# Other due times for the small products of attention, and a first down product that may begin with one block

## The chip, the cores and the metric

The kernel runs on one core of a Trainium2 chip. The metric is the device time of one execution in microseconds (us); the profiles show what each engine of that core did: TensorE (PE), VectorE (DVE), ScalarE (ACT), GpSimd (POOL) and SyncE (SP), which issues most transfers. PE runs matrix products into PSUM, which has eight banks of 2 KB per partition; one 128x512 float32 tile fills one.

## The reference

Two layers of a decoder trunk over 256 tokens of width 2048, in float32:

```python
h = rms_norm(x, norm1_g[l])
z = h @ w_in[l]                      # 2048 -> 3584: sgu u | sgu v | q | k | v
z_sgu = gelu(z[..., :2048])
out_a = chunked_sgu(z_sgu, ...)      # v normed per head, 128x128 causal mixing, times u
out_b = swa_sink_attention(q, k, v, ...)   # 16 heads of 64, 4 kv heads, window 128, sinks
mixed = concat([rms_norm(out_a), rms_norm(out_b)])
x = x + mixed @ w_out[l]
h2 = rms_norm(x, norm2_g[l])
x = x + (silu(h2 @ w_gate[l]) * (h2 @ w_up[l])) @ w_down[l]    # 2048 -> 5632 -> 2048
```

## The kernel before

**Products.** Every large product is done three times in a reduced form of float32 so that it keeps float32's precision: `mm3` multiplies the high part of the activations by the high part of the weights, then high by low, then low by high (lines 124 to 126). A weight tile `raw` (128x1024, 512 KB) comes by a transfer on SP into one of seven buffers; ACT casts its high part `wh` (line 94), DVE subtracts to get the low part `wl` (line 95). A `unit` is one such tile and its 12 products of 128x512. All engines work through their queues in order.

**Small work.** Between the units stands small work: transposes on PE (line 188; `ps_t`, `ps_f`, `ps_n` are their PSUM tiles), norms, attention and gating. `later(delay, fn)` puts a function on a list, due at the present `clock` plus the delay; every unit ends with `tick()`, which moves the clock on by one (by 0.5 for a unit of `seven`) and calls what is due, sorted by due time and then by the order in which it was put there. So the delays are the places of small work in the order of the program. A scheduler then settles the order of each engine within what the data allow.

**Banks.** Five PSUM banks are accumulators `acc` (pool `pa`), two are `dacc` (`pd`), one is `sm` (`pm`). Small work asks for a bank through `small_ps`, which takes sm, dacc, dacc, acc in turn. A bank that is asked for again comes free when its last reader, on DVE or ACT, is done.

**Attention.** `attend` makes the scores of one group of heads in two banks (`ps_s0`, `ps_s1`, line 332), which DVE scales and biases into `s` (line 337). One tick later `exps` runs on ACT (lines 353 and 357), later `turn` transposes the probabilities in two more banks (`ps_p`, line 369; ACT copies them to `pt`, line 370), and `weigh` multiplies by the values (`ps_v`, line 381). Six such groups, three for each half of the heads, start at the ticks of `UNIT_AT` (6, 9, 12, 15, 19, 23). `attend_end` transposes a half's output and splits it into `aT` (ACT line 178, DVE line 179). `q_norm` transposes queries in two steps `to_T(0)`, `to_T(1)`. `v_gate` gives the gelu of a half of v (line 434), its squares (line 207), sums on DVE (lines 213 and 169), a power on POOL (line 171), the scaling by it on DVE (lines 439 and 440) and then two spatial products (`ps_g`, line 425). Exp and gelu lie in different function tables of ACT, and a change of table shows as ACT_TABLE_LOAD.

**The feed-forward part.** Ten of eleven blocks of 512 columns go through `seven`, a scheme with seven products of blocks for eight, whose units end in the banks m0 to m4 (all of pool `pa`); ACT's Silu (line 660) and a product on DVE (line 661) then make the two halves m0 and c21 of the block, which are transposed (`ps_f`) and split into `aT` (lines 588 and 589). Block 0 goes through `gate_up`, and all blocks through `down`, in chunks of two or three blocks (`CHUNK`). These two form the second stream, `std_stream`, whose units are mixed with those of `seven` in a fixed ratio of 300 half units to 88 units less a tail of 16. `down` takes its start from the residual: `seed` copies `xres` into a `dacc` bank. When layer 0 ends, `norm_block` transposes the new residual for layer 1.

Of the kernel before, what the change touches and what calls it, by code (L numbers as in the profile page):

```python
# [39 lines left out]
NFF = DFF // NB  # L40
# [3 lines left out]
CHUNK = (2, 3)  # L44
# [19 lines left out]
def trunk(ctx, tc, x, xt, w_in, w_out, w_gate, w_up, w_down, sgu_w, sgu_g, consts,  # L64
# [182 lines left out]
    for lay in range(L):  # L247
# [40 lines left out]
        def q_norm(b, acc, lay=lay, layer=layer, qT=qT):  # L288
            qn = []
            for t in range(NTOK):  # L290
                z = zp.tile([P, NB], F32, tag="z", name="zq")
                nc.scalar.activation(z, acc[t], AF.Copy, scale=layer["rstd1"][t])
                qn.append(z)

            def scaled(inv):
                for t in range(NTOK):
                    z3 = qn[t].rearrange("p (h d) -> p h d", d=HD)
                    nc.vector.tensor_tensor(z3, z3, bc(inv[t], HD), ALU.mult)

            head_inv(qn, 8, scaled)  # L300

            def to_T(c):
                ps = transpose_pair([qn[t][:, 2 * c * P : (2 * c + 2) * P] for t in range(NTOK)])
                nc.scalar.activation(
                    qT[b][:, 2 * c : 2 * c + 2, :], ps, AF.Copy,
                    scale=cst[:, lay, C_QG : C_QG + 1],
                )

            for c in range(2):
                later(4 + c, lambda c=c: to_T(c))  # L310

        ssb = small([P, NTOK, 2], "ssb")
        ob = {}
# [8 lines left out]
        def attend(gp, t, i0, n, zkv=zkv, kT=kT, qT=qT, ob=ob, bias=bias, layer=layer):  # L322
            nk = (t + 1) * P
            nh = 2 * n
            isl = slice(i0, i0 + n)
            nsink = layer["nsink"].rearrange("p (g i) -> p g i", i=GRP)[:, 2 * gp : 2 * gp + 2, isl]
            s = ap.tile([P, 2, n, nk], F32, tag="spt", name="s", bufs=4)
            ps = [small_ps([P, n, nk], f"ps_s{r}") for r in range(2)]
            for i in range(n):
                for r in range(2):  # L330
                    rows = slice(HD * r, HD * r + HD)
                    nc.tensor.matmul(  # L332
                        ps[r][:, i, :], qT[gp][rows, i0 + i, t * P : (t + 1) * P], kT[rows, gp, :nk],
                        start=True, stop=True,
                    )
            for r in range(2):
                nc.vector.scalar_tensor_tensor(
                    s[:, r], ps[r], 1.0 / math.sqrt(HD), bias[2 * gp + r][:, isl, SEQ - nk :],
                    ALU.mult, ALU.add,
                )  # L340

            def row(name):
                return small([P, 2 * GRP], name)[:, :nh].rearrange("p (r i) -> p r i", r=2)

            m, nm, es, den, rden = (row(v) for v in ("m", "nm", "es", "den", "rden"))
            nc.vector.tensor_reduce(m, s, AX.X, ALU.max)
            nc.vector.scalar_tensor_tensor(nm, m, -1.0, nsink, ALU.mult, ALU.min)
            nc.vector.tensor_tensor(es, nm, nsink, ALU.subtract)

            def exps():  # L350
                for r in range(2):
                    for i in range(n):
                        nc.scalar.activation(
                            s[:, r, i], s[:, r, i], AF.Exp, bias=nm[:, r, i : i + 1],
                            accum_out=den[:, r, i : i + 1],
                        )
                nc.scalar.activation(es, es, AF.Exp)

            s8 = s.rearrange("p r i (b k) -> p (r i b) k", k=P)

            pts = []

            def turn():
                pt = ap.tile([P, 8, P], F32, tag="spt", name="pt", bufs=4)
                pts.append(pt)
                for half in range(2):
                    pst = small_ps([P, 4, P], "ps_p")
                    for i in range(4):
                        nc.tensor.transpose(pst[:, i, :], s8[:, 4 * half + i, :], ident)
                    nc.scalar.copy(pt[:, 4 * half : 4 * half + 4], pst)  # L370

            def weigh():
                pt = pts[0]
                nc.vector.tensor_tensor(rden, den, es, ALU.add)
                nc.vector.reciprocal(rden, rden)
                pv = small_ps([P, 2, n, HD], "ps_v")
                for r in range(2):
                    cols = slice((NKV + 2 * gp + r) * HD, (NKV + 2 * gp + r + 1) * HD)
                    for i in range(n):
                        for b in range(t + 1):  # L380
                            nc.tensor.matmul(  # L381
                                pv[:, r, i], pt[:, (r * n + i) * (t + 1) + b, :], zkv[b][:, cols],
                                start=b == 0, stop=b == t,
                            )
                if (gp, t) not in ob:
                    ob[gp, t] = zp.tile([P, NB], F32, tag="z", name="ob")
                o4 = ob[gp, t].rearrange("p (r i d) -> p r i d", r=2, d=HD)[:, :, isl]
                nc.vector.tensor_tensor(
                    o4, pv, rden.unsqueeze(3).to_broadcast([P, 2, n, HD]), ALU.mult
                )  # L390

            later(1, exps)
            later(3, turn)
            later(5, weigh)

        def attend_end(gp, r, lay=lay, ob=ob, ssb=ssb, pairs_b=pairs_b):
# [9 lines left out]
        def v_gate(b, acc, lay=lay, layer=layer, gate=gate):  # L406
            wm = ap.tile([P, 8, P], F32, tag="big", name="wm", bufs=8)
            with tc.issue_after(layer["anchor"].ins):
                nc.gpsimd.dma_start(wm, sgu_w[lay, :, 8 * b : 8 * b + 8, :])
            nc.gpsimd.affine_select(  # L410
                out=wm, in_=wm, pattern=[[0, 8], [1, P]], compare_op=ALU.is_ge, fill=0.0,
                base=0, channel_multiplier=-1,
            )
            gb = zp.tile([P, NB], F32, tag="z", name="gb")
            nc.gpsimd.dma_start(gb, sgu_g[lay, b * NB : (b + 1) * NB].partition_broadcast(P))

            v = ap.tile([P, NTOK, NB], F32, tag="big", name="v", bufs=8)
            vh = v.rearrange("p c (h d) -> p h c d", d=HD)
            gate[b] = v

            def spatial(half):
                hs = slice(4 * half, 4 * half + 4)
                ps = small_ps([P, 4, NTOK, HD], "ps_g")
                for h in range(4):
                    nc.tensor.matmul(
                        ps[:, h], wm[:, 4 * half + h, :], vh[:, 4 * half + h],
                        start=True, stop=True,
                    )
                sb = cst[:, lay, C_SB + 8 * b + 4 * half : C_SB + 8 * b + 4 * half + 4]
                for t in range(NTOK):  # L430
                    nc.vector.tensor_tensor(vh[:, hs, t], ps[:, :, t], bc(sb, HD), ALU.add)

            for t in range(NTOK):
                nc.scalar.activation(v[:, t], acc[t], AF.Gelu, scale=layer["rstd1"][t])

            def scaled(inv):
                for t in range(NTOK):
                    v3 = v[:, t].rearrange("p (h d) -> p h d", d=HD)
                    nc.vector.tensor_tensor(v3, v3, bc(inv[t], HD), ALU.mult)
                    nc.vector.tensor_tensor(v[:, t], v[:, t], gb, ALU.mult)  # L440

            head_inv([v[:, t] for t in range(NTOK)], 8, scaled)
            for half in range(2):
                later(6 + half, lambda half=half: spatial(half))

        ssa = small([P, NTOK, 2], "ssa")
        pairs_a = []
# [80 lines left out]
        for i, (gp, t, i0, n) in enumerate(units):  # L528
            at = UNIT_AT[i]
            later(at, lambda gp=gp, t=t, i0=i0, n=n: attend(gp, t, i0, n))  # L530
            if i % 3 == 2:
                if gp == 0:
                    for g in range(2, NKV):
                        later(at, lambda g=g: load_bias(g))
                for r in range(2):
                    later(at + 6 + r, lambda gp=gp, r=r: attend_end(gp, r))
        layer["anchor"] = anchor[0]
        q_norm(1, in_block(5))
        for b in range(2):
# [144 lines left out]
                yield from seven(b)  # L684

        seeds = []

        def even(b, w, lay=lay, pairs2=pairs2):
            acc = new_acc(pd, "dacc")
# [4 lines left out]
                    yield True  # L694
            return acc

        def gate_up(b, even=even, act_later=act_later, seeds=seeds):
            acc = yield from even(b, w_gate)
            sg = []
            for t in range(NTOK):  # L700
# [4 lines left out]
            for t in range(NTOK):  # L705
                nc.vector.scalar_tensor_tensor(
                    sg[t], acc[t], rstd2[t], sg[t], ALU.mult, ALU.mult
                )
                later(1.5 + 0.5 * t, lambda t=t: seeds[0](0, t))
            act_later(b, sg)  # L710

        left = [NFF]

        accs = {}
        full = {}
# [69 lines left out]
        def std_stream(gate_up=gate_up, down=down, pairs_f=pairs_f, left=left):  # L785
            gus = list(GU_BLOCKS)
            downed = set()
            while left[0]:
                full = [b for b in sorted(pairs_f) if len(pairs_f[b]) == 2 and b not in downed]
                rest = left[0] == len(full)  # L790
                if len(full) >= CHUNK[0] or rest:
                    blocks = full[: CHUNK[1]]
                    downed.update(blocks)
                    yield from down(blocks)
# [104 lines left out]
```

## Time and profile before

| | us |
|---|---|
| median of 3 runs | 1940.1 (1939.55 to 1940.67) |
| the profiled execution | 1940.95 |
| its span | 1939.2 |
| PE busy | 1925.2 |
| DVE busy | 1660.9 |
| ACT busy | 1301.4 |

The mean granted clock of PE was 0.999. A row of the timeline is: start, duration, engine, line, operation, output <- input with sizes; in brackets the idle time ahead of it and what ended it. Products are pipelined, so PE's rows overlap: a product shown with 0.39 us starts 0.23 us after the one ahead of it. Layer 0 covers about the first half of the span, layer 1 the second; attention of layer 0 lies between 60 and 165 us, of layer 1 between 1030 and 1130.

### The profile page before, as it was taken

How to read it: one execution, taken by the hardware profiler on the slowest of the kernel's cores; microseconds unless marked ns; L12 is line 12 of the kernel's file. 1: busy time of each engine (PE TensorE's matmuls, PEld its weight loads, DVE VectorE, ACT ScalarE, POOL GpSimd, SP SyncE). 2: the span in 40 equal slices, each digit the busy share in tenths (PEclk: the TensorE clock that was granted, in tenths of full speed). 3: DMA queues.
4: the chain of work that ended last, by engine and by line, in shares of the span. 5: the costliest groups of instructions: out<-in, count | busy, mean ns of one | idle time of the engine just before them, and what ended most of it. 6: DMA issues, size and time to landing. Idle time of an engine off the chain costs nothing.

```text
span 1939.2 us, 25050 instructions
## 1 busy us (share of the span) xinstructions
PE 1925.2 (99%) x8836; PEld 1578.4 (81%) x8836; DVE 1660.9 (86%) x1752; ACT 1301.4 (67%) x1729; POOL 123.2 (6%) x124
## 2 busy tenths in 40 slices
PE   9999999999999999999999999999999999999999
PEld 7888887878888888888887888878788888888887
DVE  6666689999999999999556666899999999999993
ACT  7665566667766776767755655666677767767675
POOL 1210000000000000000002000000000000000000
PEclk9999999999999999999999999999999999999999
DMA  9644558667867787777655445586678677876783
GB/s 369 201 145 158 183 168 259 215 212 243 277 212 239 225 274 213 243 238 256 196 201 192 133 163 176 176 265 209 212 237 286 208 240 226 269 218 234 238 264 125
DMA packets 118958, 426.41 MB, mean 220 GB/s; under 512 B 13232, under 2 KB 13872, under 8 KB 118832
## 3 DMA queue, kind: packets, MB, share of 16 engines
q1 hardware_dynamic: 105264, 375.52, 53.3%
q0 software_dynamic: 13568, 49.29, 14.2%
q8 instruction: 69, 1.13, 0.2%
q14 instruction: 57, 0.47, 0.1%
HBM read 422.66 MB, written 2.10 MB: 219 GB/s over the span
## 4 chain that ended last, share of the span: by engine, by line
PE 94%; issue 2%; DVE 2%; ACT 1%; POOL 0%; DMA 0%; SPq 0%; ACTq 0%; DVEq 0%; POOLq 0%
PE m L125 13%; PE m L124 13%; PE m L126 13%; PE acc L124 9%; PE acc L126 9%; PE acc L125 9%; PE dacc L125 8%; PE dacc L124 8%; PE dacc L126 8%; PE ps_f L188 1%; DVE wl L95 1%; PE ps_v L381 1%; PE ps_n L188 1%; PE ps_s L332 1%; PE ps_t L188 0%
## 5 line engine op out<-in xcount | busy, mean ns | idle before, releaser
L94 ACT CAST wh<-raw 128x1024 fp32r<-128x1024 f32 (+1 forms) x786 | 804.1, 1049 | 455.2 <-DVE raw L636 167.4
L95 DVE TENSOR_TENSOR wl<-raw,wh 128x1024 fp32r<-128x1024 f32 (+1 forms) x786 | 936.0, 1220 | 159.5 <-PE acc L125 98.8
L124 PE MATMUL m<-wh,ext 128*128 128x512 f32 x640 | 251.9, 395 | 0.6 <-ACT wh L94 0.6
L125 PE MATMUL m<-wl,ext 128*128 128x512 f32 x640 | 251.8, 393 | 0.7 <-DVE wl L95 0.6
L126 PE MATMUL m<-wh,ext 128*128 128x512 f32 x640 | 250.2, 391 | 0.0
L124 PE MATMUL dacc<-wh,aT 128*128 128x512 f32 x576 | 224.7, 391 | 0.9 <-ACT wh L94 0.9
L125 PE MATMUL dacc<-wl,aT 128*128 128x512 f32 x576 | 224.5, 390 | 0.1
L126 PE MATMUL dacc<-wh,aT 128*128 128x512 f32 x576 | 224.3, 389 | 0.0
L95 DVE TENSOR_TENSOR wl<-t,wh 128x1024 fp32r<-128x1024 f32 x160 | 194.1, 1222 | 3.7 <-issue 1.7
L94 ACT CAST wh<-t 128x1024 fp32r<-128x1024 f32 x160 | 167.9, 1052 | 38.3 <-DVE t L637 12.8
L125 PE MATMUL m<-wl,hT 128*128 128x512 f32 x480 | 187.2, 390 | 0.0
L126 PE MATMUL m<-wh,hT 128*128 128x512 f32 x480 | 186.8, 389 | 0.0
L124 PE MATMUL m<-wh,hT 128*128 128x512 f32 x480 | 186.5, 389 | 0.0
L124 PE MATMUL acc<-wh,hT 128*128 128x512 f32 x448 | 179.7, 402 | 1.3 <-ACT wh L94 1.3
L125 PE MATMUL acc<-wl,hT 128*128 128x512 f32 x448 | 175.5, 392 | 0.3 <-DVE wl L95 0.3
L126 PE MATMUL acc<-wh,hT 128*128 128x512 f32 x448 | 175.8, 392 | 0.0
L642 POOL DMA_DIRECT2D t<-in_w_gate_dram x80 | 68.4, 855 | 1331.3 <-DVE wl L95 1126.9
L124 PE MATMUL acc<-wh,aT 128*128 128x512 f32 x384 | 151.6, 395 | 0.0
L126 PE MATMUL acc<-wh,aT 128*128 128x512 f32 x384 | 150.0, 391 | 0.0
L125 PE MATMUL acc<-wl,aT 128*128 128x512 f32 x384 | 149.5, 389 | 0.0
L125 PEld LDWEIGHTS m<-wl,ext 128*128 128x128 f32 x640 | 120.2, 188 | 32.6 <-DVE wl L95 8.5
L124 PEld LDWEIGHTS m<-wh,ext 128*128 128x128 f32 x640 | 120.2, 188 | 27.0 <-ACT wh L94 2.6
(138 smaller groups left out, 2704.2 us busy)
## 6 DMA issues: line engine op xcount, KB each, us to landing
raw<-in_w_gate_dram SPq DMA_DIRECT2D x176, 512.0 KB, 5.8
raw<-in_w_up_dram SPq DMA_DIRECT2D x176, 512.0 KB, 5.6
raw<-in_w_down_dram SPq DMA_DIRECT2D x176, 512.0 KB, 5.0
raw<-in_w_in_dram SPq DMA_DIRECT2D x108, 512.0 KB, 4.2
t<-in_w_gate_dram POOLq DMA_DIRECT2D x80, 512.0 KB, 5.8
raw<-in_w_out_dram SPq DMA_DIRECT2D x64, 512.0 KB, 3.3
bias<-in_band_dram POOLq DMA_DIRECT2D x8, 512.0 KB, 4.8
xr<-in_xt_dram SPq DMA_DIRECT2D x8, 256.0 KB, 5.6
```

The costliest lines, as they stand in the source:

```text
L94: nc.scalar.copy(wh[:, j : j + step, :], src)
L95: nc.vector.tensor_tensor(wl[:, j : j + step, :], src, f(wh[:, j : j + step, :]), ALU.subtract)
L124: nc.tensor.matmul(acc, ah, wh, start=first, stop=False, skip_group_check=again)
L125: nc.tensor.matmul(acc, ah, wl, start=False, stop=False, skip_group_check=again)
L126: nc.tensor.matmul(acc, al, wh, start=False, stop=last, skip_group_check=again)
L188: nc.tensor.transpose(ps[:, j, t * P : (t + 1) * P], blocks[t][:, j * P : (j + 1) * P], ident)
L332: nc.tensor.matmul(ps[r][:, i, :], qT[gp][rows, i0 + i, t * P : (t + 1) * P], kT[rows, gp, :nk], start=True, stop=True,)
L381: nc.tensor.matmul(pv[:, r, i], pt[:, (r * n + i) * (t + 1) + b, :], zkv[b][:, cols], start=b == 0, stop=b == t,)
L642: nc.gpsimd.dma_start(t2, w_gate[lay, b, i, 1], accum_op=ALU.add)
```

## The change

Five due times move, and the start of `down` is eased. The first transposes of q come one tick earlier (3 instead of 4; the second stay at 5). `turn` is due at 2.95 instead of 3, so that in a shared tick it stands ahead of `attend` and `attend_end`. The second `attend_end` of a half comes two ticks after the first instead of one. The spatial products are due at 5 and 8 instead of 6 and 7. The first chunk of `down` may have one block (then at least two), and `gate_up` asks for a seed only while no block has gone down yet.

```diff
             for c in range(2):
-                later(4 + c, lambda c=c: to_T(c))
+                later(3 + 2 * c, lambda c=c: to_T(c))
...
             later(1, exps)
-            later(3, turn)
+            later(2.95, turn)
             later(5, weigh)
...
             for half in range(2):
-                later(6 + half, lambda half=half: spatial(half))
+                later(5 + 3 * half, lambda half=half: spatial(half))
...
                 for r in range(2):
-                    later(at + 6 + r, lambda gp=gp, r=r: attend_end(gp, r))
+                    later(at + 6 + 2 * r, lambda gp=gp, r=r: attend_end(gp, r))
...
         seeds = []
+        left = [NFF]
...
-                later(1.5 + 0.5 * t, lambda t=t: seeds[0](0, t))
+                later(1.5 + 0.5 * t, lambda t=t: left[0] < NFF or seeds[0](0, t))
             act_later(b, sg)
-
-        left = [NFF]
...
-                if len(full) >= CHUNK[0] or rest:
+                if len(full) >= (CHUNK[0] if downed else 1) or rest:
```

The products, casts and transfers are the same in number. ACT has four table loads more in all, 18 instead of 14. The chunks of `down` were blocks 0 and 1, 2 and 3, 4 and 5, 6 and 7, 8 and 9, 10; they are 1 alone as soon as `gate_up` is done, then 0 and 2, 3 and 4, 5 and 6, 7 and 8, 9 and 10.

Where instructions move, first on PE in layer 1, in the tick where the third group's scores meet the second group's `turn` (`zq` are normed queries). Before:

```order
4584 L332 MATMUL ps_s0_9090<-kT_8382,qT0_8383 128x256
4585 L332 MATMUL ps_s1_9091<-kT_8382,qT0_8383 128x256
4586 L188 MATMUL ps_t_9110<-ident_103,zq_8950 128x128
4587 L188 MATMUL ps_t_9110<-ident_103,zq_8952 128x128
4588 L188 MATMUL ps_t_9110<-ident_103,zq_8950 128x128
4589 L188 MATMUL ps_t_9110<-ident_103,zq_8952 128x128
4590 L369 MATMUL ps_p_9117<-ident_103,s_8978 128x128 x4
4591 L369 MATMUL ps_p_9123<-ident_103,s_8978 128x128 x4
4592 L124 MATMUL acc0_8958<-wh_9131,hT_8371 128x512
```

The same place on PE in the changed kernel:

```order
4586 L369 MATMUL ps_p_9096<-ident_103,s_8991 128x128 x4
4587 L369 MATMUL ps_p_9102<-ident_103,s_8991 128x128 x4
4588 L332 MATMUL ps_s0_9109<-kT_8392,qT0_8393 128x256
4589 L332 MATMUL ps_s1_9110<-kT_8392,qT0_8393 128x256
4590 L332 MATMUL ps_s0_9109<-kT_8392,qT0_8393 128x256
4591 L332 MATMUL ps_s1_9110<-kT_8392,qT0_8393 128x256
4592 L124 MATMUL acc0_8958<-wh_9131,hT_8335 128x512
```

The transposes of the probabilities stand ahead of the scores, and those of the queries are one tick earlier.

Next on ACT in layer 0, around the first `v_gate` (`s` are scores under exp, `v` the gelu's result, `sq` its squares, `void` squares of the attention's output `ob`). Before:

```order
83 L370 COPY pt_1010<-ps_p_1017 128x512
84 L353 ACTIVATE s_989,den_1005<-s_989,nm_1003 128x128 x8
85 L357 ACTIVATE es_1004<-es_1004 128x8
86 L434 ACT_TABLE_LOAD
87 L434 ACTIVATE v_1055<-acc0_740,ir2_423 128x512
88 L434 ACTIVATE v_1055<-acc1_741,ir2_423 128x512
89 L207 ACTIVATE sq_1058<-v_1055 128x512
90 L207 ACTIVATE sq_1060<-v_1055 128x512
91 L195 ACTIVATE void_1119,ssb_127<-ob_851 128x512
```

The same place on ACT in the changed kernel:

```order
84 L370 COPY pt_989<-ps_p_996 128x512
85 L434 ACT_TABLE_LOAD
86 L434 ACTIVATE v_1055<-acc0_740,ir2_423 128x512
87 L353 ACT_TABLE_LOAD
88 L353 ACTIVATE s_1002,den_1018<-s_1002,nm_1016 128x128 x8
89 L357 ACTIVATE es_1017<-es_1017 128x8
90 L434 ACT_TABLE_LOAD
91 L434 ACTIVATE v_1055<-acc1_741,ir2_423 128x512
92 L207 ACTIVATE sq_1058<-v_1055 128x512
93 L207 ACTIVATE sq_1060<-v_1055 128x512
```

The first gelu moved ahead of the eight exps, with table loads on both sides of them; layer 1 has the same.

Last on PE in layer 0, where `down` meets the end of a block of `seven` (`ps_f` transposes its m0 and c21, `dacc` is the accumulator of `down`). Before, at its first product:

```order
1744 L126 MATMUL m0_3622<-wh_3634,hT_2130 128x512
1745 L188 MATMUL ps_f_3684<-ident_103,m0_3489 128x128
1746 L124 MATMUL m1_3623<-wh_3646,ext_2101 128x512
1747 L124 MATMUL dacc0_3600<-wh_3668,aT_3619 128x512
1748 L124 MATMUL dacc1_3612<-wh_3668,aT_3619 128x512
1749 L125 MATMUL m1_3623<-wl_3647,ext_2101 128x512
```

In the changed kernel, after the same block of `seven`:

```order
1768 L126 MATMUL m0_3666<-wh_3678,hT_2094 128x512
1769 L124 MATMUL m1_3667<-wh_3690,ext_2101 128x512
1770 L188 MATMUL ps_f_3726<-ident_103,m0_3489 128x128
1771 L124 MATMUL dacc0_3703<-wh_3710,aT_3173 128x512
1772 L125 MATMUL m1_3667<-wl_3691,ext_2101 128x512
```

Here the block already has its second column of `down` in hand: it uses an `aT` made earlier, and the accumulator was seeded by a turn-over of the first column.

More of the change, by code (lines that the diff above doesn't have):

```diff
@@ L695, in even, with gate_up @@
             return acc
-        def gate_up(b, even=even, act_later=act_later, seeds=seeds):
+        def gate_up(b, even=even, act_later=act_later, seeds=seeds, left=left):
             acc = yield from even(b, w_gate)
```

## The prediction

> **What bounds the kernel now.** I read the busy table and the chain of the page first. Then came the waits of TensorE (PE), the windows of the stretches in which it loses time, and the timeline row by row at the places that the change touches.
>
> ```profile
> span 1939.2 us, 25050 instructions
> PE 1925.2 (99%) x8836; PEld 1578.4 (81%) x8836; DVE 1660.9 (86%) x1752; ACT 1301.4 (67%) x1729; POOL 123.2 (6%) x124
> PE 94%; issue 2%; DVE 2%; ACT 1%; POOL 0%; DMA 0%; SPq 0%; ACTq 0%; DVEq 0%; POOLq 0%
> ```
>
> PE is the bound, nearly everywhere: 99% busy, 94% of the chain that ended last. The change leaves the number of its products as it is, so only PE's idle or slow moments can move. The steady pitch follows from one clean run in layer 0 (T, the start of the first of these rows, is used again below):
>
> ```profile
> 106.38 0.48 PE L124 MATMUL acc<-wh,hT 128*128 128x512 f32 x1
> 106.69 0.39 PE L125 MATMUL acc<-wl,hT 128*128 128x512 f32 x1
> 111.70 0.39 PE L126 MATMUL acc<-wh,hT 128*128 128x512 f32 x1
> ```
>
> From 106.69 to 111.70 lie 22 steps in 5.01 us, 0.228 us each. Where PE loses time (window; its length, PE's busy time; granted clock):
>
> ```profile
> 60.00:165.00 105.00, 105.00 (x593) 1.00 0.49 164
> 395.00:425.00 30.00, 28.75 (x131) 1.00 0.60 209
> 1040.00:1065.00 25.00, 22.85 (x120) 0.93 0.52 168
> 1065.00:1100.00 35.00, 33.92 (x200) 1.00 0.37 121
> 1365.00:1390.00 25.00, 23.75 (x108) 1.00 0.53 195
> PE ps_p L369 <- DVE s L337: 2.1, 1, 2.1
> PE ps_s L332 <- DVE aT L179: 1.1, 1, 1.1
> ```
>
> Layer 0's attention (60 to 165) loses nothing that a window shows. Layer 1's (1040 to 1100) loses 2.15 and 1.08 us idle, and its clock drops. The first down products (395 to 425, 1365 to 1390) lose 1.25 us each.
>
> **Part 1, layer 1's attention: the five banks.** In one tick s0, s1, ps_t and both halves of ps_p are asked for, so the fifth takes the bank of the first and waits for its reader:
>
> ```profile
> 1055.95 0.60 PE L369 MATMUL ps_p<-ident,s 128*128 128x128 f32 x4
> 1058.70 0.63 PE L369 MATMUL ps_p<-ident,s 128*128 128x128 f32 x4 [2.15 <-DVE s L337]
> 1059.91 0.63 PE L124 MATMUL acc<-wh,hT 128*128 128x512 f32 x1
> 1063.28 0.39 PE L126 MATMUL acc<-wh,hT 128*128 128x512 f32 x1
> 1089.19 1.13 PE L332 MATMUL ps_s<-kT,qT 64*128 64x256 f32 x8 [1.07 <-DVE aT L179]
> 1055.93 2.03 DVE L95 TENSOR_TENSOR wl<-raw,wh 128x1024 fp32r<-128x1024 f32 x1
> 1057.88 1.27 DVE L337 SCALAR_TENSOR_TENSOR s<-ps_s,bias 128x512 f32<-128x512 f32 x2
> 1058.00:1062.00 4.00, 3.30 (x12) 0.72 0.92 251
> ```
>
> The reader L337 stood behind a subtraction of 2.03 us, so PE waited 2.15. After that the clock fell: from 1059.91 to 1063.28 are 8 steps of 0.421 instead of 0.228, 1.55 us more. In the new order ps_p stands ahead of the scores, ps_t stands in another tick, and nothing asks for a fifth bank: both terms go. The other wait, 1.07, is for the bank of an aT transpose; `attend_end`'s second half moves off that tick, and it goes too. What they covered is late next: nothing of layer 1 that isn't already so in layer 0, whose same stretch runs clean. Gain 2.15 + 1.55 + 1.07 = 4.8 us. Bounds: 1.07 + 2.15 = 3.2 if the clock finds another cause, 4.8 if all goes.
>
> **Part 2, both layers: ScalarE (ACT) at the first v_gate.** The order of ACT moves here, and this is the cost I see. Before, ACT has:
>
> ```profile
> 108.41 0.40 ACT L353 ACTIVATE s<-s,nm 128x128 f32<-128x128 f32 x1 [1.05 <-DVE nm L347]
> 111.51 0.19 ACT L357 ACTIVATE es<-es 128x8 f32<-128x8 f32 x1
> 111.72 1.28 ACT L434 ACT_TABLE_LOAD   x1
> 113.01 1.27 ACT L434 ACTIVATE v<-acc,ir 128x512 f32<-128x512 f32 x2
> 116.40 2.92 POOL L171 TENSOR_TENSOR ir<-ms,mhalf 128x16 f32<-128x16 f32 x1 [14.41 <-DVE ms L169]
> 121.56 0.48 DVE L179 SCALAR_TENSOR_TENSOR aT<-ps_t,cst,aT 128x256 fp32r<-128x256 f32 x1
> 125.39 1.89 PE L381 MATMUL ps_v<-zkv,pt 128*128 128x64 f32 x16
> ```
>
> Eight exps, es, one table, both gelus. After, the first gelu comes ahead of the exps, so table loads stand on both sides: gelu, table, eight exps, es, table, second gelu. The first gelu can't begin before its accumulator's last product, T + 5.2. The second then begins at T + 5.2 + 0.7 (half of the row of 1.27) + 1.28 + 3.10 (108.41 to 111.51) + 0.2 + 1.28 = T + 11.8. Now it begins at 113.65, which is T + 7.3. That such interleaving costs its full length, a row of the second v_gate shows: there the tables already stand on both sides of exps.
>
> ```profile
> 141.59 0.69 ACT L434 ACTIVATE v<-acc,ir 128x512 f32<-128x512 f32 x1 [1.84 <-PE acc L126]
> 145.79 1.28 ACT L434 ACT_TABLE_LOAD   x1
> 147.08 0.69 ACT L434 ACTIVATE v<-acc,ir 128x512 f32<-128x512 f32 x1
> ```
>
> From gelu to gelu 5.49 us, with four exps between. What hangs on the second gelu: its square (ACT), the sums and ms (DVE), the power on POOL (2.92), v times ir, and behind these in DVE's queue both aT subtractions. From 113.65 to the end of the second, 122.04, this takes 8.4; in the new order one more product of 0.69 (v times gb) stands ahead of it, 9.1. So the bank of ps_t comes free at T + 11.8 + 9.1 = T + 20.9. It is the bank that the new order gives to ps_v of that group. PE gets there at 125.39, T + 19.0, less 0.4 that it loses at that place now, T + 18.6. Wait 2.3 us. Behind the aT on DVE stand two L337 (1.27) and the wl that PE needs after ps_v, some 2.5 us, against 2.1 that PE gives it (ps_v 1.7 and two products): 0.35 late, and the next wl another 0.25. Sum 2.9 per layer; layer 0 gives 0.4 back that it lost there. Layer 0: +2.5. Layer 1: +2.9. Bounds: 0 where the group's chain runs 2.3 earlier than I work out, and 2.9 + 1.55 where the wait throttles the clock as the 2.15 did.
>
> That throttle is the term between bounds. A wait of 2.15 was followed by it, one of 1.07 wasn't. By the nearest row a wait of 2.3 costs 1.55 each time; but the 2.15 came amid narrow products (scores, two transposes, 1054.4 to 1059.1), and mine follows a run of wide ones. I take half, 0.8 per layer, both ends in the range.
>
> The Trainium skill (TensorE: Matmul & The Clock Gate, Part 1, "What's actually happening") says the clock halves after an idle window of about 3.4 us that runs freely. The row of 2.15 disagrees, unless the narrow products ahead count as idle. By the page the throttle term would be zero and the sum 1.6 us lower.
>
> Two more exps' and two more gelus' table loads in all (14 to 18 in the program) are those 4 x 1.28 us; ACT is 67% busy and pays for them only there.
>
> **Part 3, the first down product.** Now the last Silu of the block and four casts stand behind one another:
>
> ```profile
> 409.51 0.69 ACT L660 ACTIVATE c<-m,ir 128x512 f32<-128x512 f32 x1 [3.47 <-PE m L126]
> 410.62 3.89 ACT L94 CAST wh<-raw 128x1024 fp32r<-128x1024 f32 x4
> 411.46 0.33 PE L188 MATMUL ps_f<-ident,m 128*128 128x128 f32 x1 [0.44 <-DVE aT L589]
> 411.72 0.50 PE L124 MATMUL m<-wh,ext 128*128 128x512 f32 x1
> 413.73 0.50 PE L125 MATMUL m<-wl,ext 128*128 128x512 f32 x1 [0.32 <-DVE wl L95]
> ```
>
> ACT waited 3.47 us at the Silu, with casts queued behind; from the last clean product, at 410.62, to 413.73 PE did four products and a transpose (0.26): 3.11 - 4 x 0.228 - 0.26 = 1.9 us lost. With one block allowed, down begins at once after gate_up, so its casts spread out. But behind the Silu there still stand a copy of the residual (0.5) and the cast (0.95) for the first down product, which PE reaches 1.9 us after the accumulator's last product, and ACT 2.6 to 2.8 after it: 0.9 us remain. Gain 1.0 per layer, 2.0 in all; bounds 0 (same chain, other names) and 1.9 each. The seed guard only leaves out requests that would come too early.
>
> **Part 4, the ends.** With down ahead by one block, fewer products lie between the end of the seven-product stream and the transposes of its last block: nine instead of 24.
>
> ```profile
> 922.35 0.39 PE L126 MATMUL m<-wh,hT 128*128 128x512 f32 x1
> 923.90 0.75 DVE L661 SCALAR_TENSOR_TENSOR c<-c,nr,c 128x512 f32<-128x512 f32 x1
> ```
>
> The last factor is ready at 924.65; PE would come at 922.58 + 9 x 0.228 + 0.15 = 924.8. It just fits: +0.15 a layer for the shared bank, 1 a layer if that chain runs 1 us later. At layer 0's end the last chunk of two blocks spaces norm transposes by four units rather than two: -0.4, bounds 0 and -0.9. The transfers of weights are the same, in the same queue order to within a few units, and no row of PE waits for one; the bias loads on POOL go behind the second q_norm's power and are due ticks later, no term.
>
> **Sum.** Layer 0 attention +2.5, layer 1 attention +2.9 - 4.8 = -1.9, down -2.0, ends +0.3 - 0.4, throttle +1.6: +0.1 on the profiled execution of 1940.95 (span 1939.2 and 1.75 around it). That one is 0.85 above the median of the runs, 1940.1. Terms read by modelled ends come out small (a short wait hides the pipeline's overlap), most of them gains, so I set -0.6: 1939.5 us.
>
> **The rivals.** (a) The ACT order is harmless: the aT pair gets through ahead of the sums on DVE, or the bank is free. For it: ACT has slack (67%). Against it: in-order queues, and a wait of 2.3 that doesn't come from an average. Then -4.8 - 2.0 - 0.4 - 0.1 = -7.3: 1932.8, 0.20.
> (b) Slower, by one mechanism: the interleaved gelus cost more than worked out, since the later second gelu pushes the group behind it as well (its spatial product, moved from six ticks to five, asks for v scaled). If the wait of ps_v is 3.5 instead of 2.3, the throttle follows in full in both layers: 2 x (1.2 + 0.8) = +4 on the sum, 1943.5 to 1945. It decides from about 3.4 us of wait. For it: v times gb stands in the same DVE queue as ps_g's reader; against it: PE has 2.7 us of unit between ps_v and ps_g. 0.25.
> (c) The change doesn't do what it says at the down products (the wait takes another name there) and the drop of the clock moves to another narrow stretch of layer 1: -4.8 shrinks to -3.2, -2.0 to 0: +3.6 above, 1943. 0.10.
> The forecast: 0.45.
>
> **How the numbers follow.** 0.2% is 3.9 us, about what a measurement of this kernel can tell from no change: faster is below 1936.2, slower above 1944.0. The forecast's own range is 1937 to 1942 (throttle 0 or full, down 0 or 1.9). Rival (a) gives faster 0.20, and the forecast's tail a little; (b) slower in most of its 0.25, (c) same for the greater part. Faster 0.22, same 0.55, slower 0.23. The range holds (a)'s middle and most of (b): 1932.5 to 1945.0.
>
> **What would show it.** Part 1: no row of ps_p in layer 1 waits for L337, and the clock stays 1.00 from 1040 to 1065. Part 2: four table loads more, and a PE wait of about 2.3 at ps_v for the second aT L179 in each layer; if the clock there is under 0.9, the throttle term is real. Part 3: no ACT wait of 3.47 ahead of four casts; one PE wait under 1 us at the first dacc product. Part 4: ps_f of the last block without a wait. The prediction is wrong if ps_v doesn't wait, or if DVE, at 86%, loses time in the down units that the trace of before can't show.

## The result and the profile after

The changed kernel takes 1934.5 us (median of 8 runs, 1934.2 to 1935.2) against 1940.0 for the kernel before (median of 8, 1938.9 to 1940.7): a ratio of 0.9972, 95% interval 0.9962 to 0.9982. That is 5.5 us, 0.28%, faster. The forecast was 1939.5, with 0.55 on "same". The time lies in the stated range of 1932.5 to 1945.0, but not in the forecast's own, 1937 to 1942, and below the 1936.2 from which the prediction counts a kernel as faster, to which it gave 0.22. The profiled execution's span is 1933.5 us against 1939.2.

The page of the changed kernel, with the lines that answer to those of before:

```profile
span 1933.5 us, 25045 instructions
PE 1923.4 (99%) x8836; PEld 1577.7 (82%) x8836; DVE 1660.7 (86%) x1752; ACT 1306.7 (68%) x1733; POOL 123.4 (6%) x124
PE 98%; ACT 1%; DVE 1%; DMA 0%; issue 0%; ACTq 0%; SPq 0%; DVEq 0%
```

The chain that ended last now runs through PE at 98%, where it was 94%: what other engines held up has shrunk. The windows that the prediction showed of before (window; its length, PE's busy time; clock):

```profile
60.00:165.00 105.00, 105.00 (x592) 1.00 0.49 165
395.00:425.00 30.00, 29.41 (x135) 1.00 0.61 214
1040.00:1065.00 25.00, 25.00 (x145) 1.00 0.64 231
1065.00:1100.00 35.00, 35.00 (x204) 1.00 0.35 111
1365.00:1390.00 25.00, 24.39 (x115) 1.00 0.52 158
```

Layer 1's attention has no idle time and full clock. The two stretches of the first down products keep 0.6 us of idle time each, where they had 1.25.

Windows are coarse, because short waits hide in the overlap of PE's rows. Every kernel here has the same 7980 products of 512 columns, so the start of a given one can be compared between two traces, and the difference of the differences says what a stretch gained. For one profiled execution of each kernel, against the one of before, in us (minus is shorter; the stretches are products 50 to 1500, 1700 to 1960, 4190 to 4600 and 5450 to 5700):

| kernel | attention, layer 0 | first down, layer 0 | attention, layer 1 | first down, layer 1 | ratio of times to before, 95% interval |
|---|---|---|---|---|---|
| changed | -0.30 | -1.16 | -4.83 | -1.23 | 0.9972 (0.9962 to 0.9982) |
| e1 attention alone | -0.26 | +0.03 | -4.86 | +1.29 | 0.9983 (0.9973 to 0.9992) |
| e2 down alone | -0.04 | -0.84 | -1.68 | -1.20 | 0.9995 (0.9986 to 1.0005) |
| e3 without turn | -0.42 | -1.13 | -3.16 | -1.25 | 0.9980 (0.9971 to 0.9989) |
| e4 gelu late | +1.99 | -1.16 | +1.17 | -1.22 | 1.0015 (1.0006 to 1.0025) |
| e5 turn alone | +1.73 | +0.03 | -3.64 | -0.05 | 1.0001 (0.9991 to 1.0010) |
| e6 q alone | -0.06 | +0.05 | -3.56 | +1.26 | 0.9992 (0.9983 to 1.0001) |
| e7 end alone | -0.38 | +0.05 | -1.21 | -0.04 | 1.0002 (0.9993 to 1.0012) |
| e8 without spatial | -0.05 | -1.19 | -4.61 | -1.23 | 0.9973 (0.9962 to 0.9984) |
| e9 without end | +0.98 | -1.21 | -3.57 | -1.23 | 0.9985 (0.9975 to 0.9994) |
| e10 without q | +0.47 | -1.20 | -4.87 | -1.24 | 0.9975 (0.9966 to 0.9985) |
| e11 gelu later by less | +2.75 | -1.17 | -3.21 | -1.24 | 0.9993 (0.9984 to 1.0002) |

In the changed kernel, the end of layer 0 and the start of layer 1 (3600 to 4190) lose 0.3 and the end of the program 0.2. The start of the program, which no kernel here touches, took 0.2 to 1.7 us longer in the other profiles than in the one of before (1.06 in the changed kernel's), so single spans differ by that much for no reason of the change.

### The profile page after: what moved, and what is told of

It reads as the page before. It is cut to its first block, busy times and chain, and to the rows that moved or that the text cites. A ratio compares the mean times of both kernels' runs of the same rounds, so it can differ in the third digit from the quotient of the medians.

```text
span 1933.5 us, 25045 instructions
## 1 busy us (share of the span) xinstructions
PE 1923.4 (99%) x8836; PEld 1577.7 (82%) x8836; DVE 1660.7 (86%) x1752; ACT 1306.7 (68%) x1733; POOL 123.4 (6%) x124
## 3 DMA queue, kind: packets, MB, share of 16 engines
q8 instruction: 69, 1.13, 0.2%
## 4 chain that ended last, share of the span: by engine, by line
PE 98%; ACT 1%; DVE 1%; DMA 0%; issue 0%; ACTq 0%; SPq 0%; DVEq 0%
PE m L125 13%; PE m L124 13%; PE m L126 13%; PE acc L124 10%; PE acc L126 10%; PE acc L125 10%; PE dacc L124 8%; PE dacc L125 8%; PE dacc L126 8%; PE ps_v L381 1%; PE ps_f L188 1%; PE ps_s L332 1%; PE ps_t L188 1%; PE ps_n L188 1%; PE ps_p L369 1%; DVE wl L95 0%
```

## The experiments

The theory after the result: attention gains because no tick of layer 1 has PE waiting behind DVE for a bank any more, the down part gains because its casts no longer queue behind a late Silu, both add up, and the new order on ACT costs nothing because the first gelu starts earlier than the prediction had it. The rivals: the gain sits in one part alone; the order on ACT costs something that shows as no wait; and not the number of banks asked for but the engine that reads them decides.

**e1, attention alone.**

```diff
-                later(4 + c, lambda c=c: to_T(c))
+                later(3 + 2 * c, lambda c=c: to_T(c))
...
-            later(3, turn)
+            later(2.95, turn)
...
-                later(6 + half, lambda half=half: spatial(half))
+                later(5 + 3 * half, lambda half=half: spatial(half))
...
-                    later(at + 6 + r, lambda gp=gp, r=r: attend_end(gp, r))
+                    later(at + 6 + 2 * r, lambda gp=gp, r=r: attend_end(gp, r))
```

> The kernel before with the four edits of attention (q at 3 and 5, turn at 2.95, attend_end two ticks apart, spatial at 5 and 8), the feed-forward part as before. If the parts add up, as the timetable of the main products of the two traces says: layer 1's attention 4.8 us shorter, layer 0's 0.3 shorter, the stretches of the first down products as long as before; 5.0 us faster than before in all. If the gain of layer 1 hangs on the shift of the feed-forward part ahead of it: under 2 us faster.

Measured: 1937.1 us against 1940.5 beside it, 3.4 faster where 5.0 was expected. Layer 1's attention is 4.86 shorter, layer 0's 0.26, as expected of parts that add up. The first down product of layer 1 came out 1.29 us longer, though nothing was changed there. The windows of that run show a lower clock:

```profile
1376.00:1380.00 4.00, 3.24 (x10) 0.83 0.26 74
1380.00:1384.00 4.00, 4.00 (x17) 0.74 0.77 260
```

The three short waits of that place (0.44, 0.45 and 0.32, the same as in the kernel before) were followed by a lower clock here; in the profile of before they were not.

**e2, down alone.**

```diff
+        left = [NFF]
...
-                later(1.5 + 0.5 * t, lambda t=t: seeds[0](0, t))
+                later(1.5 + 0.5 * t, lambda t=t: left[0] < NFF or seeds[0](0, t))
...
-                if len(full) >= CHUNK[0] or rest:
+                if len(full) >= (CHUNK[0] if downed else 1) or rest:
```

> The kernel before with only the first chunk of one block and the guard of the seed; attention as before. If the parts add up: 1.1 us gained at each first down product, 0.2 lost at the ends, so 2.0 us faster than before, with the wait of ps_p of 2.1 us still in layer 1. Rival: the down stretch gains nothing alone and the whole 5.5 us comes from attention: no change.

Measured: 1939.4, 1.1 us below the kernel beside it, with an interval that holds no change. The stretches gained 0.84 and 1.20, and the ends lose 0.5 us here: 1.5 us in sum where 2.0 was expected. The rival of no gain without attention falls by the stretches, not by the times. The guard of the seed was not tried alone. The wait of ps_p is still there, but look at what follows it:

```profile
1058.47 0.63 PE L369 MATMUL ps_p<-ident,s 128*128 128x128 f32 x4 [2.14 <-DVE s L337]
1058.00:1062.00 4.00, 3.53 (x19) 1.00 0.98 338
```

The same wait as in the profile of before, at the same place, and the clock stays at 1.00. This is nearly all of the 1.68 us by which layer 1's attention is shorter than in the profile of before: the eight products of 0.42 us that the prediction read there take 0.23 us each here.

**e3, the changed kernel without the earlier turn.**

```diff
-            later(2.95, turn)
+            later(3, turn)
```

> The changed kernel with turn due at 3 again, so that scores stand ahead of ps_p in a shared tick and ACT has exps, table, both gelus as before (14 table loads instead of 18). At most four banks are still asked for in a tick, since q's transposes stay a tick earlier. If the order of ACT is harmless by its margin of 0.6 us: the same as the changed kernel within 0.7 us. If the four added table loads cost something that the waits don't show: 1 to 3 us faster than the changed kernel. If the order of ps_p ahead of the scores is what frees layer 1: 3.7 us slower than the changed kernel.

Measured: 1936.3, some 1.6 us slower than the changed kernel by the ratios, and none of the three cases in full. Layer 0 is as in the changed kernel. In layer 1, where ps_p stands behind the scores again with four banks asked for, the 2.15 us don't come back. What comes back is the other wait, 0.89 of the 1.67 us by which that stretch is longer than in the changed kernel (no marked wait shows the rest):

```profile
1084.41 1.10 PE L332 MATMUL ps_s<-kT,qT 64*128 64x256 f32 x6 [0.89 <-DVE aT L179]
```

So the four table loads more cost nothing that can be found: without its two, layer 0's attention, where no wait came back, is 0.12 us shorter. And the wait for aT hangs on `turn`, not on `attend_end`, to which the prediction gave it.

**e4, the second gelu's chain made later.** A second power on POOL at the first v_gate repeats ten of its columns with the same values (`pows` is 2 there and 1 elsewhere; the lines that hand it on are left out):

```diff
         anchor[0] = nc.gpsimd.tensor_tensor(r, ms, mhalf[:, :n], ALU.pow)
+        for _ in range(1 * (pows - 1)):
+            nc.gpsimd.tensor_tensor(r[:, :10], ms[:, :10], mhalf[:, :10], ALU.pow)
```

> The changed kernel with a second power of 10 columns on POOL at the first v_gate, into values that it only repeats: the scaling of v and what stands behind it on DVE starts about 2 us later, and the second subtraction of aT also stands behind the two L337 (1.3 us). If the mechanism of the prediction's Part 2 holds and only its start was 2.8 us too late: ps_v of both layers waits 2.0 to 2.8 us for the second aT L179, and each layer ends 2.5 to 4.5 us later. If the clock falls after such a wait as it did after the 2.15 us in the kernel before: about eight products of 0.42 us behind it, 1.5 us per layer of that. By the Trainium skill (TensorE: Matmul & The Clock Gate, Part 1), with its idle window of about 3.4 us, it would not fall. If the bank is not what ps_v waits for: no wait there and no change.

Measured: 1943.6, some 8 us slower than the changed kernel by the ratios. The two layers' timelines and the windows of the second (two added lines move the line numbers: L173 is the second power, L181, L339 and L383 are L179, L337 and L381 of the changed kernel):

```profile
122.49 1.96 POOL L173 TENSOR_TENSOR ir<-ms,mhalf 128x10 f32<-128x10 f32 x1
128.03 2.00 PE L383 MATMUL ps_v<-zkv,pt 128*128 128x64 f32 x16 [1.52 <-DVE s L339]
1093.38 3.55 PE L383 MATMUL ps_v<-zkv,pt 128*128 128x64 f32 x16 [2.67 <-DVE aT L181]
1092.00:1096.00 4.00, 2.62 (x13) 0.69 0.01 5
1096.00:1100.00 4.00, 4.00 (x15) 0.50 0.51 145
```

The mechanism of Part 2 is real: with DVE's end of the chain some 3 us later, ps_v waits for a bank in both layers (in layer 0 the banks fall another way: ps_v gets the one of the scores, whose reader L339 stands behind the same chain on DVE). Layer 0 lost 2.3 us against the changed kernel at full clock; its wait of 1.52 and this loss lie a little below what was expected. Layer 1 lost 6.0, since the clock went to half for more than 4 us: above the range that was expected.

**e11, the same by less** (8 columns instead of 10, so that only one half of v waits for them on DVE; the order on DVE stays that of the changed kernel).

> The changed kernel with a second power of 8 columns on POOL at the first v_gate: about 1.6 us later, and the order on DVE stays as in the changed kernel. ps_v came 0.6 us behind the end of the second aT there: with the margin the wait is 0.9 to 1.2 us in both layers, and each attention 0.9 to 2.2 us longer. A clock that falls only behind waits of about 2 us and more stays at 1.00.

Measured: 1938.7. The two waits and the windows behind them:

```profile
126.51 1.97 PE L383 MATMUL ps_v<-zkv,pt 128*128 128x64 f32 x16 [1.03 <-DVE aT L181]
1091.43 1.97 PE L383 MATMUL ps_v<-zkv,pt 128*128 128x64 f32 x16 [1.10 <-DVE aT L181]
128.00:132.00 4.00, 4.00 (x14) 0.62 0.37 131
1092.00:1096.00 4.00, 4.00 (x24) 1.00 0.32 105
```

The waits are as long as worked out from the margin. But the shorter of two like waits throttled the clock and the longer didn't: layer 0 lost 3.05 us against the changed kernel, above the 0.9 to 2.2 expected, layer 1 1.62. The supposition that the clock falls only behind waits of about 2 us and more is wrong.

**e5, turn at 2.95 alone** (the second line pair of e1's diff).

> The kernel before with turn at 2.95 alone. Five banks are still asked for in the tick of layer 1 (both halves of ps_p, s0, s1, ps_t), in another order. If what counts is which engine reads the bank that the fifth request takes: the fifth is now ps_t, on the bank of the first ps_p, whose reader is ACT's short copy; no wait over 0.5 us is left in layer 1's attention, the wait of ps_s for aT L179 included, and that stretch is 3.2 us shorter than before, 4.8 where the kernel before is throttled in it. If the number of banks counts, as the change's words say: a wait of about 2 us stays there.

Measured: 1940.2 against 1940.6, no change. In layer 1 every wait of PE at ps_p and ps_s is gone although five banks are still asked for in that tick, as the theory of the reader had it. But the edit costs something: the ACT order with the late second gelu comes with it (this edit alone makes it), and layer 0 lost 1.73 us. Its longest wait by the view of waits, and what DVE had done until then:

```profile
PE acc L125 <- DVE wl L95: 1.6, 3, 1.0
129.23 1.22 DVE L95 TENSOR_TENSOR wl<-raw,wh 128x1024 fp32r<-128x1024 f32 x1
```

In that trace DVE has no gap from 122.25 on: the scaling of v, four subtractions of aT, two L337, a reduction and `ob`, and only then, at 129.23, the low part that PE needs. Layer 1's attention is 3.64 shorter, not 4.8 as expected beside a throttled kernel: the same low part comes late there too, ending at 1094.97, and PE's product behind it starts at 1095.02.

**e6, q's transposes at 3 and 5 alone** (the first line pair of e1's diff).

> The kernel before with the transposes of q at 3 and 5 alone. Four banks are asked for in that tick (s0, s1, both halves of ps_p). If the fifth request is the cause of the 2.15 us: it goes, and with it any throttling behind it; the wait of ps_s for aT L179 (1.07 us) stays, so layer 1's attention is 2.2 to 3.7 us shorter. If the order of ps_p behind the scores is the cause: no gain.

Measured: 1938.9 against 1940.6, with an interval that just holds no change. The 2.15 us are gone with four banks and the order otherwise as before, and the other wait stays:

```profile
1086.01 1.13 PE L332 MATMUL ps_s<-kT,qT 64*128 64x256 f32 x8 [1.07 <-DVE aT L179]
```

Layer 1's attention is 3.56 shorter, of which 1.55 is the throttle that only some executions have. The first down product of layer 1 again ran throttled (+1.26).

**e7, attend_end two ticks apart alone** (the last line pair of e1's diff).

> The kernel before with the second attend_end two ticks after the first, alone. By the prediction's Part 1 this edit removes the wait of ps_s for aT L179: layer 1 about 1.1 us shorter, the 2.15 us of ps_p as before. By the run without turn, where that wait stayed at 0.9 us though this edit was in: no gain, the wait stays at 0.8 to 1.2 us.

Measured: 1940.9 against 1940.6. Both waits are there:

```profile
1059.61 0.63 PE L369 MATMUL ps_p<-ident,s 128*128 128x128 f32 x4 [2.15 <-DVE s L337]
1088.52 1.10 PE L332 MATMUL ps_s<-kT,qT 64*128 64x256 f32 x6 [0.90 <-DVE aT L179]
```

The clock stays at full behind the first of them, which accounts for the -1.21 of the table. Alone, this edit gains nothing.

**e8, the changed kernel with the spatial products at 6 and 7 again.**

> The changed kernel with the spatial products at 6 and 7 again. No wait of before hung on them, so within 0.5 us of the changed kernel in both attentions. If the move to 5 and 8 is what keeps a tick under five requests: a wait of 0.5 to 2 us at ps_g or at the scores next to it in one layer or both.

Measured: 1934.8, ratio 0.9973 against 0.9972: the move of the spatial products does nothing that can be told.

**e9, the changed kernel with attend_end one tick apart again.**

> The changed kernel with the second attend_end one tick after the first again. In the run of turn alone the second gelu came late as here and DVE then had both splits of aT, two L337, a sum and the low part of the weights in one bunch; PE waited 1.0 us for that wl in layer 0 (1.7 us lost in that attention). If the spread of attend_end is what pays for the late gelu: 2.0 to 2.5 us slower than the changed kernel in layer 0's attention and 0.8 to 1.5 in layer 1's, at the acc L125 behind ps_v and ps_g, none at ps_p. If the loss in the run of turn alone came from the fifth bank: no change, since here only four are asked for.

Measured: 1936.6, 2.5 us slower than the changed kernel by the ratios. Layer 0 lost 1.28 us against it, less than expected, and layer 1 1.26. The view of waits marks nothing of it, but PE's low product starts as soon as DVE has its low part, in both layers (here layer 0; in the changed kernel that low part starts at 126.67):

```profile
128.42 1.22 DVE L95 TENSOR_TENSOR wl<-raw,wh 128x1024 fp32r<-128x1024 f32 x1
129.69 0.50 PE L125 MATMUL acc<-wl,hT 128*128 128x512 f32 x1
```

That is the place at which e5 lost its time. The edit that gains nothing alone pays, in the whole, for what the earlier turn does to DVE.

**e10, the changed kernel with q's transposes at 4 and 5 again.**

> The changed kernel with the transposes of q at 4 and 5 again: five banks are asked for in that tick, ps_p first. If the order frees it and not the number: the attentions as in the changed kernel within 0.5 us each. If the number: a wait of 1 us or more at ps_t or at the scores.

Measured: 1935.2, ratio 0.9975. Layer 1 is as in the changed kernel with five banks asked for. Layer 0 lost 0.77 us, at the scores behind ps_p (94 to 96 us), with no wait over 0.5 us: between the two expectations there.

## Why the prediction was right or wrong

**The bound.** PE's idle and slow moments were all that moved, as predicted; its products and their pitch stayed. The time lies in the stated range, but not by the sum that led to 1939.5: the range was drawn wide enough to hold rival (a), and it is a form of that rival which came true. That the range held was luck as far as Part 2 goes.

**Part 1, layer 1's attention.** Predicted -4.8, measured -4.83 in the pair of profiles, but with two corrections. First, 1.55 of it is a throttle that comes behind the wait of 2.15 us in some executions only: of the three profiles that have this wait, one (before) shows it, two (e2, e7) don't. Without the throttle the gain is 3.3 us. Second, the prediction gave the wait of ps_s for aT to `attend_end`'s second half. Kernels with that edit but without the earlier turn keep it (e3 0.89, e7 0.90); the turn removes it, alone (e5) and without the spread (e9). Either of two edits, q's or turn's, removes the 2.15 us (e6, e5), so a fifth request is not enough for that wait: e5 and e10 make it and don't have it in layer 1.

**Part 2, ACT at the first v_gate: the step that failed.** It is the one sentence "The first gelu can't begin before its accumulator's last product, T + 5.2". The timeline of the changed kernel (PE twice, ACT, POOL, DVE, PE):

```profile
107.49 0.50 PE L124 MATMUL acc<-wh,hT 128*128 128x512 f32 x1
109.44 0.39 PE L126 MATMUL acc<-wh,hT 128*128 128x512 f32 x1
109.86 0.69 ACT L434 ACTIVATE v<-acc,ir 128x512 f32<-128x512 f32 x1 [0.87 <-PE acc L126]
116.47 0.69 ACT L434 ACTIVATE v<-acc,ir 128x512 f32<-128x512 f32 x1
119.28 2.93 POOL L171 TENSOR_TENSOR ir<-ms,mhalf 128x16 f32<-128x16 f32 x1 [17.16 <-DVE ms L169]
125.08 0.48 DVE L179 SCALAR_TENSOR_TENSOR aT<-ps_t,cst,aT 128x256 fp32r<-128x256 f32 x1
126.14 1.90 PE L381 MATMUL ps_v<-zkv,pt 128*128 128x64 f32 x16
```

T is 107.49, and the first gelu begins at T + 2.4, right behind its accumulator's last product at 109.44, the eighth after T. T + 5.2 is 2.8 us too late. It is about where the 24 products of the prediction's first run end (111.70, T + 5.3), and these are two units, of which the second is another accumulator's. It is also about where ACT was done with its exps in the kernel before (111.51 + 0.19); there both gelus stood behind these and a table load, until T + 6.6, so their start didn't show when the data were ready. Every other size of the chain held: gelu to gelu 6.6 us (116.47 - 109.86; predicted 6.6), second gelu to the end of the second aT 9.1 (125.56 - 116.47; predicted 9.1), PE at ps_v at T + 18.65 (predicted 18.6). So the bank came free at T + 18.1 instead of T + 20.9, 0.6 us ahead of PE instead of 2.3 behind it. The terms of +2.5 and +2.9, and +1.6 for the throttle, were not there, and ps_v didn't wait, which the prediction had named as the sign that it is wrong. e4 and e11 put 1.6 to 2 us and more into the same chain, and the waits came.

That is rival (a), "the ACT order is harmless", worked out at 1932.8, though by an earlier start and not by the reasons given there. It came out 1.7 us above that, probably because 1.55 of its 4.8 isn't in every execution, and by the ends.

**Part 3, the first down product.** Predicted -1.0 a layer with 0.9 us left; measured -1.16 and -1.23, with this left:

```profile
413.69 0.59 ACT L745 COPY xres<-dacc 128x512 f32<-128x512 f32 x1 [3.76 <-PE dacc L126]
416.26 0.69 ACT L660 ACTIVATE c<-m,ir 128x512 f32<-128x512 f32 x1
416.84 0.58 ACT L745 COPY xres<-dacc 128x512 f32<-128x512 f32 x1
417.30 1.06 ACT L94 CAST wh<-raw 128x1024 fp32r<-128x1024 f32 x1
418.42 0.50 PE L124 MATMUL dacc<-wh,aT 128*128 128x512 f32 x1 [0.59 <-ACT wh L94]
```

ACT still has a long wait, 3.76 us, but the Silu is now followed by a copy, one cast and another copy (418.25), no longer by four casts in a row. Silu, copy and cast stand in a row as predicted, and PE waits 0.59 us for the cast. Right, to 0.2 us a layer. One thing was not foreseen: of the ten first down products in the five profiles without this edit (before, e1, e5, e6, e7) two ran at a lower clock and took 1.3 us more, of the sixteen in the eight profiles with it none.

**Part 4, the ends.** Predicted +0.3 - 0.4; measured +0.3 at the end of layer 0 and +0.2 at the end of the program. The transposes of the last block come without a marked wait, as worked out. The gain of 0.4 at layer 0's norms didn't show.

**The sum.** What was measured in the one profile of each, without the throttle: -0.3 (layer 0's attention), -3.3, -2.4, +0.3, +0.2, together -5.5 us. The medians differ by as much. How far that is chance one profile each can't tell, since the start of the program and the throttle differ by 1 to 2 us from one execution to the next.

**The throttle.** "By the nearest row a wait of 2.3 costs 1.55 each time": no. Waits of 2.14 and 2.15 us at the same place were followed by it once in three profiles, waits of 1.03 and 1.10 in e11 once in two, six others of 0.89 to 1.07 (before, e2, e3, e5, e6, e7) not, one of 1.52 not, one of 2.67 for more than 4 us. By the Trainium skill (TensorE: Matmul & The Clock Gate, Part 1) the window in which activity is counted runs freely and isn't restarted by the kernel; that two like waits of e11 went two ways fits this and doesn't show it. By the same section of the Trainium skill it takes an idle window of about 3.4 us; here a wait of 1.03 us between narrow products was enough. What of the narrow products counts as idle, no run here shows.

## What to carry to other kernels

When a reordering puts an instruction ahead of others on an engine, work out when its input is ready from the producer's queue, down to the one product that ends the accumulator (here the ninth and not the 24th of a run): the old start of the instruction may be the engine's, not the data's. Count the margin that is left at the end of such a chain (here 0.6 us): some 1.6 us more ahead of it made a wait of 1.0 us (e11). Edits that gain nothing alone can pay together: neither the earlier turn nor the spread of attend_end did alone, and with q's move and that of the spatial products they gained 3.4 us (e1). A bank asked for too often costs what its reader's queue costs: five requests cost 2.15 us behind a busy VectorE in layer 1, and no wait there in another order (e5, e10).

## What the runs showed of the hardware

The clock of TensorE fell behind waits as short as 1.03 us, and behind three waits of 0.3 to 0.45 us within 3 us, but only sometimes: two like waits in one execution went two ways. Each time it cost 1.3 us and more, up to some 3 us behind the wait of 2.67. A kernel that is 99% busy can so lose or gain a microsecond or two from one execution to the next. The eight runs of the kernel before, which has more of these waits, spread over 1.8 us, those of the changed kernel over 1.1; that the throttle makes the difference isn't shown.

A switch of ACT's function table took 1.28 us and the next instruction began right behind it (from the gelu's row, whose end is at 110.55, to the first exp at 111.87); four more of them in the program cost nothing that e3 can show (0.12 us in layer 0's attention).
